# Low parts of whole weight rows by accumulating DMA, and products with the low part last, in a decoder layer on one core

## The chip, the core and the metric

The kernel runs on one core of a Trainium2 chip. The core has TensorE (matrix products into PSUM; PE in the rows), VectorE (DVE), ScalarE (ACT) and GpSimd (POOL), each with an instruction queue of its own, and SyncE (SP), which issues plain transfers. Transfers are carried by 16 DMA engines. The metric is the time of one execution on the device in microseconds (us).

## The reference

It is one step of one decoder layer, for 512 prompt tokens and 8 sample tokens that share their weights. Cut to its products:

```python
x = x + 0.5 * swiglu(rmsnorm(x, norm_ffn1), w_ffn1_gate, w_ffn1_up, w_ffn1_down)
z = rmsnorm(x, norm_mix) @ w_in
...  # RWKV-7 time mixing y_a, short convolution y_b, gates g_a and g_b, all from z
x = x + (g_a * y_a + g_b * y_b) @ w_out
x = x + 0.5 * swiglu(rmsnorm(x, norm_ffn2), w_ffn2_gate, w_ffn2_up, w_ffn2_down)
x = x + jax.nn.sigmoid(rmsnorm(x, norm_ple) @ w_ple_gate) * (p @ w_ple_proj)
```

Everything is float32; the model's width is 1024, that of the FFN 2816. A last norm follows.

## The kernel before

Tokens lie along the free dimension: 520 columns, handled as two halves of 260. The residual `X` is eight tiles of 128 x 520. A product's weights are blocks of 128 x 128; a whole row of 8 blocks is 128 x 1024 and takes in all of the model's width for 128 outputs.

**Three matmuls for one.** Float32 is worked out of two parts of TensorE's faster type fp32r: hi (rounded) and lo (what the rounding left). `mm3` (L171 to L173) does hi x h, hi x l and lo x h for one block, h and l being the parts of the activations (`xh`, `xl`; `xsh`, `xsl`; `th`, `tl`). A half of a product over a whole row is 8 blocks x 3 = 24 matmuls of 260 columns into one PSUM bank (`big`).

**How the parts are made.** `load` brings a row or block to `raw` through SP (L120). `make` (L122 to L132) then has two ways. With an engine in `eng`, ACT copies raw to hi (L130) and that engine subtracts: lo = raw - hi (L132). Without one, ACT writes -raw to lo (L128), a DMA that GpSimd issues adds the weights to it from HBM (L129), which leaves what the rounding of -raw lost, and ACT makes hi from raw.

**Whole rows.** `Row` is such a block of 128 x 1024; its raw, hi and lo tiles have two buffers each (tags raw8, hi8, lo8). `plain` (L212) builds a product from two units, one for each half of the columns; where the product is as deep as one row (`nk == NT`, 8 blocks) it uses one `Row`. These are wg1[1] and wu1[0 and 1] of FFN 1 (wg1[0] is prepared by hand in a tile of its own), w_out's rows 2 to 7, wg2[0 and 1] and wu2[0 and 1] of FFN 2, and the 8 rows of w_ple_gate (wpg): 21 in all. The other pairs of FFN rows go through `seven`, seven products of sums of blocks in place of eight; they take the sums `ts`, `th`, `tl` of the activations (`sums4`, L305 to L321), made by ACT and VectorE while the first products of an FFN run.

**What sets the order.** `run` (L184) walks through the units: it issues loads and `make` steps up to LEAD = 10 units ahead as the buffers allow, then a unit's matmuls, then what uses its result. Within this, a scheduler orders each engine's instructions by priorities and data. In FFN 1 and 2 the first result needs the norm's factors: `rstd` (L346) sums the squares on TensorE (`nsum`, L349), takes the root on ACT (`nR`, L350, behind a load of ACT's table) and the reciprocal on VectorE (L351).

Of the kernel before, what the change touches and what calls it, by code (L numbers as in the profile page):

```python
# [17 lines left out]
NT = 8  # L18
# [3 lines left out]
HN = N // 2  # L22
# [34 lines left out]
def hybrid_step(tc, I, O):  # L57
    nc = tc.nc
    from contextlib import ExitStack

    with ExitStack() as top:
# [34 lines left out]
        HALF = (slice(0, HN), slice(HN, N))  # L96
# [71 lines left out]
        def mm3(ps, b, i, x, first, last):  # L168

            hi, lo = b.hi[:, i, :], b.lo[:, i, :]  # L170
            nc.tensor.matmul(ps[:, :HN], lhsT=hi, rhs=x[0], start=first, stop=False, skip_group_check=True)  # L171
            nc.tensor.matmul(ps[:, :HN], lhsT=hi, rhs=x[1], start=False, stop=False, skip_group_check=True)  # L172
            nc.tensor.matmul(ps[:, :HN], lhsT=lo, rhs=x[0], start=False, stop=last, skip_group_check=True)  # L173
# [38 lines left out]
        def plain(pool, src, x, consume, mk=fps, lo_eng=None):  # L212

            nk = src.shape[1]
            if nk == NT:
                bs = [Row(src, nc.vector)]
            else:
                bs = [Blk(pool, src[:, k:min(k + KH, nk)], lo_eng) for k in range(0, nk, KH)]
            got = {}

            def half(j):
                def emit():
                    got[j] = mk("big")
                    k = 0
                    for b in bs:
                        for i in range(b.n):
                            a = x(k)
                            mm3(got[j], b, i, (a[0][:, HALF[j]], a[1][:, HALF[j]]), k == 0, k == nk - 1)
                            k += 1
                return emit  # L230
            n = len(bs)
            row = nk == NT
            if row:
                n = 0
            us = [Unit(half(0), lambda: consume(got[0][:, :HN], HALF[0]), bs, [b.make for b in bs], -n, n, 0, (row, row, row, 0)),
                  Unit(half(1), lambda: consume(got[1][:, :HN], HALF[1]), free=n, rows=(0, 0, 0, row))]
            for u in us:
                u.used = consume
            return us
# [146 lines left out]
        def ffn(fp, wg, wu, wd, XS, TS, R, htile, post):  # L386
# [79 lines left out]
            def down(m, k0, n, mk=mwps):  # L466
                last = k0 + n == NF

                def on_d(ps, cs):
                    nc.vector.scalar_tensor_tensor(X[m][:, cs], ps, 0.5, X[m][:, cs], ALU.mult, ALU.add)  # L470
                    if last and m == NT - 1:
                        post(m, cs)
                    elif last and cs.start:
                        post(m, ALL)
                return plain(fp, wd[m][:, k0:k0 + n], lambda k: hs[k0 + k], on_d, mk, nc.vector if k0 == 0 and m < KH else None)

            units, downs = [], []
            for q in range(NPAIR):
                f = 2 * q
                if q == 0:  # L480
                    parts = [plain(fp, w[f + i], lambda k: XS[k], on(q, i)) for w, on in ((wg, on_g1), (wu, on_u1)) for i in range(2)]
                else:
                    parts = [seven(fp, w[f], w[f + 1], XS, TS, on(q), nc.vector if q == 1 else None) for w, on in ((wg, on_g), (wu, on_u))]
                for x in parts:
                    units += x
                    if q:
                        for _ in range(2):
                            if downs:
                                units += downs.pop(0)
                if q % 2 and q < NPAIR - 3:  # L490
                    downs += [down(m, f - 2, 4) for m in range(NT)]
                elif q == NPAIR - 2:

                    downs += [down(m, f - 2, 4) for m in range(KH)]
# [151 lines left out]
        with tc.tile_pool(name="f2", bufs=1) as fp:  # L646
# [50 lines left out]
            def plains(w, x, on):  # L697
                us = [u for m in range(NT) if w[m] is not None
                      for u in plain(fp, w[m], x, lambda ps, cs, m=m: on(ps, cs, m))]
                us[-1].now = us[-2].now = True  # L700
                return us
# [779 lines left out]
```

## Time and profile before

| what | value |
|---|---|
| time, median of 3 runs | 1517.29 us (1516.64 to 1518.45) |
| the profiled execution | 1518.29 us, of which its span is 1516.5 |
| mean granted clock of TensorE | 0.977 of full speed |
| busy share of the span: TensorE, VectorE, ACT, GpSimd | 95%, 71%, 51%, 26% |
| FFN 1, the mix, w_out, FFN 2, wpg begin at about | 5, 350, 1044, 1090, 1453 us |

The span runs from the first to the last instruction; the 1.8 us beside it belong to the launch. The profiled execution is 1.0 us above the median of the runs.

### The profile page before, as it was taken

Reading aid. Unit: us, or ns where it says so; the run is one execution under the profiler, and the core shown is the slowest. Engines: PE = TensorE matmul, PEld = TensorE weight load, DVE = VectorE, ACT = ScalarE, POOL = GpSimd, SP = SyncE. Lnnn points to the kernel's source line nnn. Section 1 sums busy time; section 2 is a strip of 40 time slices with the busy share of each in tenths; the row PEclk is TensorE's granted clock in tenths of the full one; section 3 lists DMA queues with packets and bytes.
Section 4 is the critical chain, followed back from the end, with each engine's and each line's share of the span. In section 5 each row is a group of like instructions: output and inputs, shape, how many; then the busy total and the mean of one; then the engine's idle time right before and its main releaser. Section 6 shows DMA issues by size and latency. Waiting matters only on the chain.

```text
span 1516.5 us, 36191 instructions
## 1 busy us (share of the span) xinstructions
PE 1446.9 (95%) x14772; PEld 1390.4 (92%) x14772; DVE 1076.5 (71%) x2349; ACT 770.1 (51%) x1352; POOL 398.5 (26%) x447
## 2 busy tenths in 40 slices
PE   8799999999999999999899999998989999999996
PEld 7799999999988988989888897898979999999996
DVE  7976665665698877859887659855697665666566
ACT  7655555555633443634444352244475555555643
POOL 1324334334231211201320113311023334333401
PEclk9899999999998999999999999999999999999998
DMA  5678888888332322313222222325246887888823
GB/s 180 153 167 182 181 183 183 182 191 181 123 106 68 82 66 53 97 45 83 67 67 66 73 78 87 100 88 168 91 125 161 178 185 176 192 180 172 169 68 103
DMA packets 116709, 193.44 MB, mean 128 GB/s; under 512 B 41992, under 2 KB 51208, under 8 KB 116288
## 3 DMA queue, kind: packets, MB, share of 16 engines
q1 hardware_dynamic: 92928, 140.80, 30.4%
q0 software_dynamic: 23616, 50.34, 20.7%
q8 instruction: 116, 1.90, 0.5%
q14 instruction: 49, 0.40, 0.1%
HBM read 179.83 MB, written 11.01 MB: 126 GB/s over the span
## 4 chain that ended last, share of the span: by engine, by line
PE 75%; DVE 15%; ACT 3%; issue 3%; DMA 2%; POOL 1%; SPq 0%; DVEq 0%; ACTq 0%; POOLq 0%
PE big L171 16%; PE big L173 16%; PE big L172 16%; PE big L795 6%; PE big L796 6%; PE big L797 5%; DVE lo L132 2%; PE xy L1171 1%; PE ds L1186 1%; PE xy L1177 1%; ACT hi L130 1%; PE ft L1123 1%; PE xy L1154 1%; DVE F L1090 1%; ACT W L1127 1%
## 5 line engine op out<-in xcount | busy, mean ns | idle before, releaser
L130 ACT ACTIVATE hi<-raw 128x512 fp32r<-128x512 f32 (+2 forms) x427 | 318.5, 749 | 323.6 <-PE big L172 171.2
L795 PE MATMUL big<-xh,hi 128*128 128x260 f32 x1040 | 310.5, 299 | 1.7 <-ACT cc L847 1.0
L797 PE MATMUL big<-xh,lo 128*128 128x260 f32 x1040 | 299.6, 289 | 2.0 <-DVE lo L132 2.0
L796 PE MATMUL big<-xl,hi 128*128 128x260 f32 x1040 | 300.8, 289 | 0.0
L132 DVE TENSOR_TENSOR lo<-raw,hi 128x512 fp32r<-128x512 f32 (+2 forms) x263 | 239.2, 912 | 62.1 <-ACT hi L130 57.0
L795 PEld LDWEIGHTS big<-xh,hi 128*128 128x128 f32 x1040 | 199.8, 192 | 11.6 <-ACT cc L847 1.2
L171 PE MATMUL big<-hh,hi 128*128 128x260 f32 x704 | 203.6, 289 | 3.0 <-DVE x L470 3.0
L797 PEld LDWEIGHTS big<-xh,lo 128*128 128x128 f32 x1040 | 199.3, 192 | 4.2 <-DVE lo L132 2.3
L796 PEld LDWEIGHTS big<-xl,hi 128*128 128x128 f32 x1040 | 200.1, 192 | 2.8
L172 PE MATMUL big<-hl,hi 128*128 128x260 f32 x704 | 199.5, 283 | 0.0
L173 PE MATMUL big<-hh,lo 128*128 128x260 f32 x704 | 199.5, 283 | 0.0
L171 PE MATMUL big<-th,hi 128*128 128x260 f32 x640 | 183.1, 286 | 8.5 <-ACT th L319 5.2
L172 PE MATMUL big<-tl,hi 128*128 128x260 f32 x640 | 182.8, 286 | 3.6 <-DVE tl L320 3.4
L173 PE MATMUL big<-th,lo 128*128 128x260 f32 x640 | 181.8, 284 | 0.0
L470 DVE SCALAR_TENSOR_TENSOR x<-big,x 128x260 f32<-128x260 f32 x176 | 74.5, 426 | 94.9 <-PE big L173 94.9
L171 PEld LDWEIGHTS big<-hh,hi 128*128 128x128 f32 x704 | 133.3, 189 | 6.5 <-DVE x L470 3.5
L173 PEld LDWEIGHTS big<-hh,lo 128*128 128x128 f32 x704 | 133.3, 189 | 0.0
L172 PEld LDWEIGHTS big<-hl,hi 128*128 128x128 f32 x704 | 133.2, 189 | 0.0
L171 PEld LDWEIGHTS big<-th,hi 128*128 128x128 f32 x640 | 121.5, 190 | 10.1 <-ACT th L319 6.0
L172 PEld LDWEIGHTS big<-tl,hi 128*128 128x128 f32 x640 | 121.6, 190 | 4.8 <-DVE tl L320 4.8
L171 PE MATMUL big<-xh,hi 128*128 128x260 f32 x400 | 114.9, 291 | 8.4 <-ACT hi L130 5.5
L166 DVE TENSOR_TENSOR raw<-raw 128x512 f32<-128x512 f32 x160 | 113.9, 713 | 12.6 <-DMA raw<-in_wu 5.6
(306 smaller groups left out, 3439.4 us busy)
## 6 DMA issues: line engine op xcount, KB each, us to landing
raw<-in_win SPq DMA_DIRECT2D x66, 512.0 KB, 3.8
raw<-in_wd SPq DMA_DIRECT2D x80, 256.0 KB, 2.9
lo<-in_wd POOLq DMA_DIRECT2D x72, 256.0 KB, 4.6
raw<-in_wu SPq DMA_DIRECT2D x24, 512.0 KB, 3.7
raw<-in_wg SPq DMA_DIRECT2D x23, 512.0 KB, 3.8
raw<-in_wg SPq DMA_DIRECT2D x40, 256.0 KB, 3.5
raw<-in_wu SPq DMA_DIRECT2D x40, 256.0 KB, 3.0
lo<-in_wg POOLq DMA_DIRECT2D x18, 512.0 KB, 5.7
```

Of the source, the lines that this page charges most:

```text
L130: nc.scalar.activation(self.hi[:, ks], self.raw[:, ks], AF.Identity)
L132: self.eng.tensor_tensor(self.lo[:, ks], self.raw[:, ks], self.hi[:, ks].bitcast(F32), ALU.subtract)
L166: nc.vector.tensor_tensor(self.raw, a.raw, b.raw, ALU.add)
L171: nc.tensor.matmul(ps[:, :HN], lhsT=hi, rhs=x[0], start=first, stop=False, skip_group_check=True)
L172: nc.tensor.matmul(ps[:, :HN], lhsT=hi, rhs=x[1], start=False, stop=False, skip_group_check=True)
L173: nc.tensor.matmul(ps[:, :HN], lhsT=lo, rhs=x[0], start=False, stop=last, skip_group_check=True)
L470: nc.vector.scalar_tensor_tensor(X[m][:, cs], ps, 0.5, X[m][:, cs], ALU.mult, ALU.add)
L795: nc.tensor.matmul(ps[:, :HN], lhsT=hi[:, k, :], rhs=hh[k][:, cs], start=k == 0, stop=False)
L796: nc.tensor.matmul(ps[:, :HN], lhsT=hi[:, k, :], rhs=hl[k][:, cs], start=False, stop=False)
L797: nc.tensor.matmul(ps[:, :HN], lhsT=lo[:, k, :], rhs=hh[k][:, cs], start=False, stop=k == nk - 1)
L1090: v1.tensor_tensor(f, f, ft[:, :, q0:, :j], ALU.add)
L1123: nc.tensor.matmul(ps[qd, i * 128:i * 128 + 96], lhsT=GM[qd, i, 96:], rhs=GM[qd, i, 0:96], start=False, stop=True, skip_group_check=True)
```

## The change

Two edits in `plain`, for products over a whole row alone. The `Row` gets no engine, so that its low part comes from ACT's copy of -raw and the accumulating DMA. And a half's 24 matmuls are written as 16 with the hi part (hi x h and hi x l for each of 8 blocks) and then 8 with the low part, in place of hi, hi, lo for each block. The number of matmuls is the same.

```diff
--- before.py
+++ after.py
@@ -213,7 +213,7 @@
 
             nk = src.shape[1]
             if nk == NT:
-                bs = [Row(src, nc.vector)]
+                bs = [Row(src)]
             else:
                 bs = [Blk(pool, src[:, k:min(k + KH, nk)], lo_eng) for k in range(0, nk, KH)]
             got = {}
@@ -221,6 +221,15 @@
             def half(j):
                 def emit():
                     got[j] = mk("big")
+                    if row:
+
+                        for part in range(2):
+                            for k in range(NT):
+                                h, l = (y[:, HALF[j]] for y in x(k))
+                                for w, r in (((bs[0].hi, h), (bs[0].hi, l)), ((bs[0].lo, h),))[part]:
+                                    nc.tensor.matmul(got[j][:, :HN], lhsT=w[:, k, :], rhs=r, start=part == k == 0 and r is h,
+                                                     stop=part == 1 and k == NT - 1, skip_group_check=True)
+                        return
                     k = 0
                     for b in bs:
                         for i in range(b.n):
```

Line numbers behind the second edit are 9 higher in the changed kernel (L304 there is L295 here). Numbers behind an underscore count tiles, and those of the two kernels differ.

**ACT at the start of FFN 1.** hi_164 and lo_165 are the parts of wg1[1]; hi_220 and lo_221 (before), or 221 and 222 (changed), those of wu1[0]; `nsq` are squares for the norm. Before:

```order
L130 ACTIVATE hi_164<-raw_135 128x1024
L342 ACTIVATE nsq_151<-x5_71 128x520
L130 ACTIVATE hi_220<-raw_162 128x1024
L342 ACTIVATE nsq_154<-x6_72 128x520
L342 ACTIVATE nsq_157<-x7_73 128x520
L350 ACT_TABLE_LOAD
L350 ACTIVATE nR_96<-nsum_256,vec_74 128x260
L350 ACTIVATE nR_96<-nsum_260,vec_74 128x260
L130 ACTIVATE hi_318<-raw_168 128x1024
```

With the change:

```order
L128 ACTIVATE lo_165<-raw_135 128x1024
L130 ACTIVATE hi_164<-raw_135 128x1024
L351 ACTIVATE nsq_151<-x5_71 128x520
L128 ACTIVATE lo_222<-raw_162 128x1024
L351 ACTIVATE nsq_154<-x6_72 128x520
L130 ACTIVATE hi_221<-raw_162 128x1024
L351 ACTIVATE nsq_157<-x7_73 128x520
L359 ACT_TABLE_LOAD
L359 ACTIVATE nR_96<-nsum_258,vec_74 128x260
L359 ACTIVATE nR_96<-nsum_262,vec_74 128x260
L130 ACTIVATE hi_320<-raw_169 128x1024
L128 ACTIVATE lo_321<-raw_169 128x1024
```

A copy for the low part now stands ahead of the one for hi, in the place that hi had, and two more such copies stand ahead of the norm's table load and of te.

**TensorE at the start of FFN 1.** The first matmuls of the second product (wg1[1]), whose two halves are big_230 and big_280 before, big_232 and big_282 with the change. Before:

```order
L171 MATMUL big_230<-xh0_97,hi_164 128x260
L172 MATMUL big_230<-xl0_98,hi_164 128x260
L171 MATMUL big_280<-xh0_97,hi_164 128x260
L172 MATMUL big_280<-xl0_98,hi_164 128x260
L173 MATMUL big_230<-xh0_97,lo_165 128x260
L171 MATMUL big_230<-xh1_99,hi_164 128x260
L172 MATMUL big_230<-xl1_100,hi_164 128x260
L173 MATMUL big_230<-xh1_99,lo_165 128x260
```

With the change, the last 2 of big_232's 16 hi matmuls and what follows them:

```order
L230 MATMUL big_232<-xh7_111,hi_164 128x260
L230 MATMUL big_232<-xl7_112,hi_164 128x260
L230 MATMUL big_282<-xh0_97,hi_164 128x260
L230 MATMUL big_282<-xl0_98,hi_164 128x260
L230 MATMUL big_282<-xh1_99,hi_164 128x260
L230 MATMUL big_282<-xl1_100,hi_164 128x260
L230 MATMUL big_282<-xh2_101,hi_164 128x260
L230 MATMUL big_232<-xh0_97,lo_165 128x260
L230 MATMUL big_232<-xh1_99,lo_165 128x260
```

And further on in the changed kernel, up to the norm's sums:

```order
L230 MATMUL big_232<-xh6_109,lo_165 128x260
L230 MATMUL big_232<-xh7_111,lo_165 128x260
L230 MATMUL big_282<-xl2_102,hi_164 128x260
L230 MATMUL big_282<-xh3_103,hi_164 128x260
L230 MATMUL big_282<-xl3_104,hi_164 128x260
L230 MATMUL big_282<-xh4_105,hi_164 128x260
L230 MATMUL big_282<-xl4_106,hi_164 128x260
L230 MATMUL big_282<-xh5_107,hi_164 128x260
L358 MATMUL nsum_258<-nss_95,vec_74 128x260
L358 MATMUL nsum_262<-nss_95,vec_74 128x260
```

Low parts were read from the fifth matmul of the product on; now 21 hi matmuls of both halves stand ahead of the first. The norm's sums stand behind 37 matmuls of the product before, and behind 35 with the change, 8 of them with the low part.

**ACT at the start of w_out.** hi_14409 (before) or hi_14412 (changed) is the hi part of w_out's row 2, hi_14415 or hi_14419 that of row 3; xsh and nsq are parts and squares of the residual. Before:

```order
L130 ACTIVATE hi_14409<-raw_14405 128x1024
L295 ACTIVATE xsh_14377<-x0_14199,vec_74 128x260 x2
L342 ACTIVATE nss_14375<-x0_14199 128x520
L295 ACTIVATE xsh_14377<-x1_14223,vec_74 128x260 x2
L342 ACTIVATE nsq_14398<-x1_14223 128x520
L130 ACTIVATE hi_14415<-raw_14407 128x1024
L295 ACTIVATE xsh_14379<-x2_14243,vec_74 128x260
```

With the change:

```order
L130 ACTIVATE hi_14412<-raw_14408 128x1024
L304 ACTIVATE xsh_14380<-x0_14202,vec_74 128x260 x2
L351 ACTIVATE nss_14378<-x0_14202 128x520
L304 ACTIVATE xsh_14380<-x1_14226,vec_74 128x260 x2
L351 ACTIVATE nsq_14401<-x1_14226 128x520
L128 ACTIVATE lo_14413<-raw_14408 128x1024
L128 ACTIVATE lo_14420<-raw_14410 128x1024
L130 ACTIVATE hi_14419<-raw_14410 128x1024
L130 ACTIVATE hi_14479<-raw_14417 128x1024
L304 ACTIVATE xsh_14382<-x2_14246,vec_74 128x260
```

The low copies of rows 2 and 3 stand between the squares and the hi copy of row 3. In TensorE's order, row 2's 32 hi matmuls are followed by 14 with hi_14419 and then by row 2's 16 with lo_14413; before, the low parts of row 2 were read from its fifth matmul on.

**ACT at the start of FFN 2.** hi_14885 (before) or hi_14896 (changed) is the hi part of wg2[1], hi_14985 that of wu2[0]; te begins the sums of the activations. Before:

```order
L130 ACTIVATE hi_14885<-raw_14738 128x1024
L350 ACT_TABLE_LOAD
L350 ACTIVATE nR_14376<-nsum_14864,vec_74 128x260
L350 ACTIVATE nR_14376<-nsum_14868,vec_74 128x260
L312 ACTIVATE te_14876<-x0_14199,vec_74 128x520
L312 ACTIVATE te_14876<-x4_14283,vec_74 128x520
L408 ACT_TABLE_LOAD
L408 ACTIVATE t_14863<-t_14863 128x520
L319 ACTIVATE th_14873<-ts_14875 128x1040
```

With the change:

```order
L130 ACTIVATE hi_14896<-raw_14748 128x1024
L128 ACTIVATE lo_14897<-raw_14748 128x1024
L359 ACT_TABLE_LOAD
L359 ACTIVATE nR_14379<-nsum_14875,vec_74 128x260
L359 ACTIVATE nR_14379<-nsum_14879,vec_74 128x260
L130 ACTIVATE hi_14985<-raw_14822 128x1024
L321 ACTIVATE te_14887<-x0_14202,vec_74 128x520
L321 ACTIVATE te_14887<-x4_14286,vec_74 128x520
L417 ACT_TABLE_LOAD
L417 ACTIVATE t_14874<-t_14874 128x520
```

A low copy has come in ahead of the table load, and hi_14985, which waits for a buffer of hi, stands ahead of te; before, the hi copy of that row (hi_14973) came later than the rows shown. VectorE's subtractions for these rows are gone from its order, and the sums' tl stand behind fewer subtractions and sums of blocks than before.

## Rows read from the trace of the kernel before

**Rows 1.** The page's first part, TensorE's row: busy us (share of the span), instructions.

```profile
PE 1446.9 (95%) x14772; PEld 1390.4 (92%) x14772; DVE 1076.5 (71%) x2349; ACT 770.1 (51%) x1352; POOL 398.5 (26%) x447
```

**Rows 2.** Busy us by stretch (instructions in brackets), granted clock, DMA share, GB/s.

```profile
19.00:21.00 2.00, 2.00 (x19) 2.00 (x18) 1.90 (x4) 1.05 (x2) 0.00 (x0) 1.00 1.07 340
42.00:60.00 18.00, 13.81 (x76) 12.61 (x77) 16.45 (x30) 10.96 (x18) 5.50 (x5) 0.64 0.58 147
1040.00:1062.00 22.00, 18.54 (x141) 18.13 (x140) 11.34 (x21) 8.67 (x14) 0.00 (x0) 0.92 0.44 137
1470.00:1496.00 26.00, 26.00 (x219) 26.00 (x219) 19.06 (x31) 12.47 (x18) 0.00 (x0) 1.00 0.37 113
```

**Rows 3.** Groups by form: instruction, count | busy us, mean ns | idle before.

```profile
L132 DVE TENSOR_TENSOR lo<-raw,hi 128x1024 fp32r<-128x1024 f32 x93 | 116.5, 1253 | 37.7 <-ACT hi L130 36.3 <-PE ft L1123 0.7
L128 ACT ACTIVATE lo<-raw 128x1024 fp32r<-128x1024 f32 x36 | 37.6, 1044 | 0.6 <-PE big L173 0.6
```

**Rows 4.** Timeline, a low copy: start us, us, instruction [idle before <-releaser].

```profile
45.29 1.06 ACT L128 ACTIVATE lo<-raw 128x1024 fp32r<-128x1024 f32 x1 [0.56 <-PE big L173]
46.66 0.87 POOL L129 DMA_DIRECT2D lo<-in_wg  x1 [0.60 <-ACT lo L128]
```

**Rows 5.** The page's DMA queues and issues; accumulating landings, 0:60 and 1121:1123.

```profile
q1 hardware_dynamic: 92928, 140.80, 30.4%
q0 software_dynamic: 23616, 50.34, 20.7%
lo<-in_wg POOLq DMA_DIRECT2D x18, 512.0 KB, 5.7
...
DMA to landing us min/median/max: 4.0/4.2/6.0
...
DMA to landing us min/median/max: 7.3/7.3/7.3
```

**Rows 6.** Timeline of the start of FFN 1, same columns.

```profile
14.52 1.04 ACT L130 ACTIVATE hi<-raw 128x1024 fp32r<-128x1024 f32 x1
21.36 0.70 PE L349 MATMUL nsum<-nss,vec 128*128 128x260 f32 x2
22.61 3.41 DVE L351 RECIPROCAL nR<-nR 128x260 f32<-128x260 f32 x2 [1.31 <-ACT nR L350]
28.25 2.33 DVE L132 TENSOR_TENSOR lo<-raw,hi 128x1024 fp32r<-128x1024 f32 x1
49.33 1.24 DVE L320 TENSOR_TENSOR tl<-ts,th 128x1040 fp32r<-128x1040 f32 x1 [0.19 <-ACT th L319]
49.35 0.58 PE L171 MATMUL big<-th,hi 128*128 128x260 f32 x1 [3.17 <-ACT th L319]
```

**Rows 7.** Timeline of the start of w_out.

```profile
1048.25 1.04 ACT L130 ACTIVATE hi<-raw 128x1024 fp32r<-128x1024 f32 x1
1048.48 0.59 PE L173 MATMUL big<-xh,lo 128*128 128x260 f32 x1 [3.15 <-DVE lo L132]
1051.03 0.42 PE L172 MATMUL big<-xl,hi 128*128 128x260 f32 x1
1051.25 0.42 PE L173 MATMUL big<-xh,lo 128*128 128x260 f32 x1
1061.12 1.06 ACT L130 ACTIVATE hi<-raw 128x1024 fp32r<-128x1024 f32 x1 [1.55 <-PE big L172]
```

**Rows 8.** Timeline of the start of FFN 2.

```profile
1090.49 0.47 PE L171 MATMUL big<-xsh,hi 128*128 128x260 f32 x1
1092.77 3.41 DVE L351 RECIPROCAL nR<-nR 128x260 f32<-128x260 f32 x2 [0.57 <-ACT nR L350]
1105.26 1.21 DVE L132 TENSOR_TENSOR lo<-raw,hi 128x1024 fp32r<-128x1024 f32 x1
1122.51 0.39 PE L172 MATMUL big<-tl,hi 128*128 128x260 f32 x1 [0.89 <-DVE tl L320]
1140.81 0.39 PE L171 MATMUL big<-th,hi 128*128 128x260 f32 x1 [1.79 <-DVE u L441]
```


## The prediction

> **What bounds the kernel now.** The page's first part says it at once: TensorE's matmuls are busy 95% of the span [rows 1]. The table of busy time by stretch says where the rest is lost: in the middle of the row products nothing is (26.00 us busy of 26, 219 matmuls, so 0.119 us each), while at the starts of the stages TensorE stands still and the clock falls (a granted clock of 0.64 in 42 to 60, 0.92 in 1040 to 1062) [rows 2]. So work taken from VectorE is worth nothing in the middle of these products; it can be worth something only where TensorE waits: at the start of FFN 1, of w_out and of FFN 2. Since about 1,515 of the 1,517 us are untouched, the question is what happens at three starts, and whether the new transfers keep up in between.
>
> **The pieces and their prices.** Removed: 21 subtractions of 128x1024 on VectorE, 1253 ns each (26 us). Added: 21 ACT copies of 128x1024, 1044 ns each (22 us) [rows 3], and 21 accumulating transfers of 512 KB issued by GpSimd. Neither total is on the path by itself: VectorE is busy 71% of the span and ACT 51%. What counts is how long a low part takes from its raw row. Before, ACT copy and VectorE subtraction: 1.04 + 1.22 us. After: the ACT copy of -raw, a lag of 0.31 us to GpSimd's issue (46.66 against 45.29 + 1.06) [rows 4], and the landing. For 512 KB the page gives a median of 5.7 us from issue; singly I see 4.0 to 6.0 in the first 60 us and 7.3 in a busy stretch [rows 5]. I take 5.7, or 6.0 where other loads run beside it, and keep 4.0 and 7.3 as ends. Then a low part is there about 7.1 us after its ACT copy starts, 4.8 us later than before. The new order hides 16 of a half's 24 matmuls (1.9 us) of that; prefetching must hide the rest.
>
> A sentence from the Trainium skill bears on this price ("DMA: Bandwidth & Descriptors", section "Anatomy of one DMA — SWDGE (gpsimd) path"): it fits such a transfer as 2.0 us plus its bytes over 436 thousand per us, from which I work out an estimate of 3.2 us for 512 KB. The trace's 5.7 us does not agree; by the page, low parts would come some 2.5 us earlier and the sum below would be that of the second rival.
>
> **A, start of FFN 1.** Product 0 is untouched. Of product 1, 37 matmuls stand ahead of the norm's sum in the order of before, 35 in that of the change, but 14 of these come behind the first low part. Before: the sum ran at 21.36, and VectorE's reciprocal, from which a nearly gapless VectorE chain runs to the last tl at 49.33, began at 22.61; TensorE then still waited 3.17 us at 49.35 for that chain [rows 6]. After: ACT makes lo_165 at the place where it made hi (14.52), so it ends at 15.57 and the transfer is issued at 15.9; with 6.0 us it lands at 21.9 (the DMA engines are all taken from 19 to 21: share 1.07 [rows 2]). hi_164 comes at 16.6, just as product 0 ends. TensorE does 21 matmuls of it, to 16.6 + 21 x 0.12 = 19.1, and waits 2.8 us. After a wait of 3.15 us at w_out the next 13 matmuls came 0.216 us apart, the step of 1.2 GHz [rows 7]; I price the 14 matmuls here so: 3.0 us. The sum runs at 24.9, 3.5 us late, and so does the VectorE chain. That chain has lost one subtraction (28.25, 2.33 us, the usual price 1.22): 1.7 between. A = 3.5 - 1.7 = **+1.8 us**. Ends: a landing of 4.0 gives 19.9, a short wait, no fall of the clock, the sum 0.2 late, A = -1.5; 7.3 gives the sum 4.9 late and A = +3.7.
>
> **B, start of w_out.** Before, TensorE did 4 matmuls, waited 3.15 us for VectorE's subtraction (queued behind the residual adds) and ran 13 at half speed [rows 7]; the second product ended at about 1061.0 (the ACT copy that waits for it starts at 1061.12). After, it goes on where it stopped (1048.48 - 3.15 = 1045.3) with the 28 other hi matmuls of that product, to 1045.3 + 28 x 0.12 = 1048.7. Then it needs hi_14419, which now stands third in ACT's row, behind lo_14413 and lo_14420: 1048.25 + 3 x 1.05 = 1051.4, a wait of 2.7. The 14 matmuls that come ahead of the first low part, at 0.216, bring it to 1054.4. lo_14413 lands at 1049.3 + 0.3 + 5.7 = 1055.3: another 0.9. The 50 matmuls left take 6.0 at full clock: 1061.3, or 1062.3 if the clock stays down for some ten of them. B = **+0.8** (0.3 to 1.3); with 4.0 there is no second wait, -0.7; with 7.3 +2.5. So a stall of some 3 us is not removed: it changes its owner, from VectorE to ACT.
>
> **C, start of FFN 2.** The reciprocal starts as before (the ACT low copy stands where hi stood, and hi starts a little earlier). te, which followed the norm's scales at once, now stands behind hi_14985. This waits until the hi matmuls of the product of 1090.49 are through, 40 matmuls (4.8 us) later, and takes 1.05: te at about 1096.4. VectorE is in its reciprocals until 1096.2, so this costs it 0.4 to 0.9. It loses the subtraction of 1105.26 (1.21 us), and others move behind tl, so that the last tl, for which TensorE waited until 1122.51, comes up to 3.6 us earlier. But what was moved back must still be done: the next wait, 1.79 us at 1140.81 for VectorE's u, is gated by the whole backlog [rows 8]. I therefore count only what left the chain, and the wins at the waits: **-1.2**, between +0.5 (te's delay counts) and -2.8.
>
> **D, the rows in between.** The row tiles have two buffers. lo of product p+2 may begin when product p ends; the copy (1.05), the lag (0.3) and 0.1 of signalling leave, up to the 17th matmul of p+2 (5.76 + 1.92 = 7.7 us later), 6.2 us for the landing. 5.7 fits with half a us to spare. GpSimd does nothing else in w_out and wpg (1470 to 1496: 0.00 busy [rows 2]), so no issue is held up. DMA room: the accumulating queue took 20.7% of 16 engines for 50.34 MB, the plain one 30.4% for 140.80 MB [rows 5]; that is 6.2 us per MB against 3.3, so 3.3 us per row of 512 KB and, for a whole wpg product with its raw row (1.7) and pq (0.9), about 5.9 of 5.76 us if all ran at once; before, loads ran far ahead (share 0.37). That is tight: I add **+0.5** for a few late landings. If every one took 7.3, the cycle of a buffer (32 matmuls, 3.84, + 1.45 + 7.3 = 12.6 us for two products, not 11.52) costs 0.54 a product, over some 12 products +6.5.
>
> SP's queue hardly moves, TensorE's matmuls stay the same in number, and the end of the kernel (behind 1496) isn't touched.
>
> **Sum.** +1.8 + 0.8 - 1.2 + 0.5 = +1.9 us on the profiled execution, 1518.29 us, gives 1520.2; it ran 1.0 above the median 1517.29, so against the median I forecast **1519.2**.
>
> **The rivals.**
>
> *The transfers don't keep up* (slower): all landings like the 7.3 us: A +3.7, B +2.5, C +0.5, D +6.5, together +13, 1530; at 6.7 about half that. For it: the DMA arithmetic of D. Against: wpg moved little before, and quiet stretches gave 4.0. Beside it stands a warning of the Trainium skill ("SBUF — State Buffer", section "SBUF: two separate sides"): VectorE in its two-port modes keeps GpSimd from writing descriptors for transfers it issues; that would lengthen landings, and no row of before isolates it.
>
> *The transfers are early* (faster, the other side): decided at the start of FFN 1. If lo_165 lands within about 4.3 us of its issue, TensorE hardly waits, the clock holds, and the subtraction that left VectorE's chain is a gain: A -1.5, B -0.7, C -2.8, D 0, together -5, 1512.3. For it: two of the three landings in the first 60 us took 4.0 to 4.2. Against: those ran when the DMA engines had room, and 19 to 21 is full.
>
> *It cancels*: VectorE's spare time in 42 to 60 (1.55 us of 18) takes up most of A's delay, A about +0.3, and C gets -1.5: +0.1, 1517.4.
>
> **Chances.** A measurement of this kernel can tell about 0.2% (3 us) from no change. Forecast +1.9 (own range 1517.5 to 1522): 0.45. Late transfers: 0.17. Early ones: 0.18. Cancelling: 0.20. Of the forecast's cases a quarter pass +3 us; of the early ones some stay above -3 us, of the late ones a few below +3. So slower 0.28, same 0.55, faster 0.17. For 8 in 10 the range takes in the early case (1512.3) almost whole and the milder half of the late one: 1512.5 to 1525.
>
> **What would show it.** A: a wait of 2 to 3 us before the 22nd hi matmul, for a DMA, the clock below full from 21 to 25, the reciprocal near 26. B: a wait for ACT's hi at about 1048.4 to 1051.4, one of 1 us for a DMA behind it. C: last tl before 1121, the wait for u still there. D: TensorE full from 1450 to 1496. The forecast is wrong if accumulating landings sit away from 5 to 6 us, if the clock doesn't fall after A's wait, or if TensorE waits in wpg.

## The result and the profile after

The change made the kernel slower: 1543.65 us (median of 6 runs, 1535.16 to 1544.17) against 1517.17 us before on the same chip, a ratio of 1.0158 (95% interval 1.0139 to 1.0176; the two medians alone give 26 us, 1.0175). The forecast, 1519.2 us with a range up to 1525, missed. The profiled execution, 1535.16 us, is the quickest of the six; a second one (`after_again`, below) took 1542.95.

The page after, first the row of the engines and the two DMA queues (columns as in [rows 1] and [rows 5]), then the accumulating transfers of the two stages that had none before:

```profile
PE 1446.6 (94%) x14772; PEld 1389.9 (91%) x14772; DVE 1053.0 (69%) x2328; ACT 789.7 (51%) x1373; POOL 416.9 (27%) x468
...
q1 hardware_dynamic: 92928, 140.80, 29.8%
q0 software_dynamic: 26640, 61.35, 24.4%
...
lo<-in_wpg POOLq DMA_DIRECT2D x8, 512.0 KB, 6.7
lo<-in_wo POOLq DMA_DIRECT2D x6, 512.0 KB, 7.9
```

TensorE is busy for as long as before, and its mean granted clock is 0.977 in both profiles; VectorE lost 23.5 us, ACT gained 19.6. So, in sum, the time lost is waiting. The first rows of TensorE's waits by what ended them, over the whole span (us in total, times, longest):

```profile
PE big L230 <- DMA lo<-in_wo: 7.8, 3, 3.1
...
PE big L230 <- DMA lo<-in_wpg: 5.7, 2, 5.6
PE big L230 <- DMA lo<-in_wg: 5.7, 2, 4.5
PE big L230 <- DMA lo<-in_wu: 5.5, 3, 2.8
```

These are 24.7 us of waits for an accumulating DMA; before there was none. The loss is smaller than that because waits of before, the 3.15 us of [rows 7] above all, are gone or shorter. Where they stand, from the timeline of TensorE (FFN 1, w_out with its ACT wait, FFN 2, wpg):

```profile
23.08 0.59 PE L230 MATMUL big<-xh,lo 128*128 128x260 f32 x1 [4.49 <-DMA lo<-in_wg]
...
1051.35 0.39 PE L230 MATMUL big<-xh,hi 128*128 128x260 f32 x1 [1.96 <-ACT hi L130]
1056.36 3.47 PE L230 MATMUL big<-xh,lo 128*128 128x260 f32 x16 [3.08 <-DMA lo<-in_wo]
1069.22 1.23 PE L230 MATMUL big<-xh,lo 128*128 128x260 f32 x8 [2.98 <-DMA lo<-in_wo]
...
1122.55 3.84 PE L230 MATMUL big<-xsh,lo 128*128 128x260 f32 x16 [2.83 <-DMA lo<-in_wu]
...
1499.59 2.10 PE L230 MATMUL big<-xs,lo 128*128 128x260 f32 x8 [5.56 <-DMA lo<-in_wpg]
```

Behind the longer waits the clock falls to the lower of its two levels, 1.2 GHz: the 16 matmuls of 1056.36 took 3.47 us, 0.22 each, and the 8 of 1499.59 2.10, where the 8 of 1069.22 took 1.23. Behind the wait of 2.98 us the fall came 1.3 us later, and behind that of 1.96 there was none. The stretches behind 1056.36 and 1069.22 (columns as in [rows 2]; the granted clock is the third number from the end):

```profile
1056.30:1060.00 3.70, 3.64 (x18) 3.61 (x18) 0.55 (x2) 0.64 (x2) 0.00 (x0) 0.57 0.90 239
1071.00:1072.00 1.00, 1.00 (x6) 1.00 (x6) 0.49 (x1) 0.46 (x1) 0.00 (x0) 0.50 0.95 209
```

By stages, from the first start of each stage's marker on TensorE (the norms' sums, the first matmul of w_out's own products in the mix, wo), in us:

| run | to FFN 1's sum | to the mix's first group sum | to wo | wo to FFN 2's sum | to wpg's sum | to the end |
|---|---|---|---|---|---|---|
| before | 21.4 | 364.8 | 645.5 | 58.1 | 369.1 | 57.6 |
| after | 26.2 | 363.4 | 642.8 | 68.8 | 366.4 | 65.8 |
| `after_again` | 26.7 | 365.0 | 646.8 | 69.9 | 366.4 | 66.4 |
| `e1_order` | 21.4 | 366.6 | 646.3 | 54.7 | 367.9 | 57.7 |

The first profile's 16.9 us are +4.8, -1.4, -2.7, +10.7, -2.7 and +8.2. The mix, which the change leaves alone, takes 642.8 to 646.8 us from one profile to the next. Of the 7.8 us between the two profiles of the changed kernel 4.0 lie there, so differences of a few us between single profiles are not put down to an edit below unless its own stage shows them.

### The profile page after: what moved, and what is told of

It reads as the page before. It is cut to its first block, busy times and chain, and to the rows that moved or that the text cites. A ratio compares the mean times of both kernels' runs of the same rounds, so it can differ in the third digit from the quotient of the medians.

```text
span 1533.4 us, 36253 instructions
## 1 busy us (share of the span) xinstructions
PE 1446.6 (94%) x14772; PEld 1389.9 (91%) x14772; DVE 1053.0 (69%) x2328; ACT 789.7 (51%) x1373; POOL 416.9 (27%) x468
## 4 chain that ended last, share of the span: by engine, by line
PE 38%; DVE 6%; issue 6%; DMA 5%; ACT 2%; POOL 1%; DVEq 0%; POOLq 0%; ACTq 0%
PE big L171 7%; PE big L172 7%; PE big L173 7%; PE big L804 4%; PE big L805 4%; PE big L806 4%; DMA lo<-in_wo 1%; DMA lo<-in_wpg 1%; PE big L230 1%; PE xy L1180 1%; PE ds L1195 1%; DVE lo L132 1%; PE xy L1186 1%; PE xy L1163 1%; DMA lo<-in_wu 1%
## 5 line engine op out<-in xcount | busy, mean ns | idle before, releaser
L804 PE MATMUL big<-xh,hi 128*128 128x260 f32 x1040 | 309.9, 298 | 1.0 <-ACT cc L856 1.0
L132 DVE TENSOR_TENSOR lo<-raw,hi 128x512 fp32r<-128x512 f32 (+2 forms) x242 | 212.8, 882 | 46.1 <-ACT hi L130 40.9
L128 ACT ACTIVATE lo<-raw 128x512 fp32r<-128x512 f32 (+2 forms) x185 | 134.7, 730 | 1.0 <-PE big L230 0.8
```

The costliest lines, as they stand in the source:

```text
L128: nc.scalar.activation(self.lo[:, ks], self.raw[:, ks], AF.Identity, scale=-1.0)
L132: self.eng.tensor_tensor(self.lo[:, ks], self.raw[:, ks], self.hi[:, ks].bitcast(F32), ALU.subtract)
L804: nc.tensor.matmul(ps[:, :HN], lhsT=hi[:, k, :], rhs=hh[k][:, cs], start=k == 0, stop=False)
```

## The experiments

Times are ratios to the kernel before on the same chip. Landing means from GpSimd's issue to the end of the transfer.

### One half of the change alone, the load held back, the change again

Theory L: the same ACT copy that starts an accumulating transfer frees the raw tile, so that a plain load starts with it, and the landing is late. The rivals: the transfer is slow by itself; or the order of the matmuls costs.

```diff
# e1_order
-                bs = [Row(src)]
+                bs = [Row(src, nc.vector)]
# e2_dma_mixed
-                    if row:
+                    if False:
# e3_hold: the make step of a whole row
+            def make_hold():
+                b = bs[0]
+                b.make()
+                nc.gpsimd.tensor_copy(b.raw[:, 0, 0:1], b.lo[:, 0, 0:1].bitcast(F32))
```

> Only the new order of the matmuls; low parts of these rows by VectorE's subtraction as before. If the accumulating transfers are the whole cost, this is not slower than before: at w_out the low part comes at 1048.4 and 28 more hi matmuls stand ahead of it, so the wait of 3.15 us shrinks to the one for ACT's hi of row 3 (about 0.6), and the 13 matmuls at half speed go: about 1513 us (1511 to 1517). If the order itself costs (the norm's sums behind more matmuls, rows of hi read sooner), it is slower than before: 1519 or more.

> Only the accumulating DMA; matmuls in the old order hi, hi, lo. If late landings are the cost, the 1.7 us that the order had hidden are lost on top: a buffer of low parts then turns in 5.76 + 1.45 + 7.5 = 14.7 us for two products, where the change needs 12.8, so about 1 us more for each of 12 products and more at the starts: 1550 to 1565 us. If the order were the cost, this is between before and the change: 1520 to 1535.

> The change, but the next plain load of a whole row starts only when the accumulating transfer has landed (GpSimd copies one column of the low part into the raw tile, after its last reader). Theory: the ACT copy that starts an accumulating transfer also frees the raw tile, so a plain load of 512 KB starts with it and takes its share of the engines; then landings in w_out and wpg fall from 7 to 8 us to 4.0 to 5.5, the DMA waits there fall under 1 us each, and the time is about 1525 us (1520 to 1530). Rival, the accumulating transfer is slow by itself in these stretches: landings stay at 7 or more, and the time at 1535 to 1545.

> The changed kernel unaltered, for a second profile, since its runs lay between 1535 and 1544 us. If the difference comes from landings, the stretch that is longer shows longer waits for the accumulating DMA (wpg, where one wait of 5.6 us stood, above all); if it comes from the mix, which gave back 4 us of FFN 1's delay in the first profile, the shift at w_out's start is 4 to 5 us here instead of 0.7.

Measured: the order alone **0.9972** (0.9961 to 0.9984), faster than before; the DMA alone **1.0332** (1.0308 to 1.0357), a median of 1568.96 us where I had expected 1550 to 1565; the load held back 1.0175 (1.0160 to 1.0190); the change again 1.0134 (1.0108 to 1.0161). The order is not the cost; it gives 4 us back. The waits in w_out (1040 to 1092) of the order alone, against [rows 7]:

```profile
PE big L230 <- DVE lo L132: 0.5, 1, 0.5
PE big L230 <- ACT hi L130: 0.3, 1, 0.3
```

The 3.15 us stall is down to 0.5, as 28 more hi matmuls cover VectorE's subtraction. And the order hides a part of the DMA's lateness: without it the DMA costs twice as much (0.0332 over before, against 0.0162 over the order alone).

Holding the load back did half of what L says. In 1062 to 1078, landings of the change and, below, of `e3_hold`:

```profile
DMA to landing us min/median/max: 7.8/8.0/8.0
```

```profile
DMA to landing us min/median/max: 5.5/5.5/5.6
```

but no time was won in all. In `e3_hold` w_out's stretch took 65.9 us, some 3 less than with the change, but the two behind it took 373.6 and 70.0, 7 and 4 more. The held loads came late themselves and lay beside later transfers (landings of up to 8.8 in wpg), and GpSimd waits for each landing in its row; how much of FFN 2's 7 us that wait is was not traced. The time is the rival's, though the landings fell as L says. So the next runs take the load away instead of moving it.

### wpg: the plain load, the buffers, ACT's row

```diff
# e4_noload: wpg's rows 2 to 7 take the raw tiles of rows 0 and 1
+                if self.like is not None:
+                    self.raw = self.like.raw
# e6_three: hi and lo of wpg in three places each (the places are left out here)
-                    if nm > i and (nm > i + LEAD or prep + m.preps > PREP or raw + m.raws > RAW or rprep + m.rows[2] > 2):
+                    if nm > i and (nm > i + LEAD or prep + m.preps > PREP or raw + m.raws > RAW or rprep + m.rows[2] > (3 if m.own else 2)):
# e10_nosq: e4_noload, and
+                    if m in (0, NT - 1):
                         nrm3.add(m, c)
# e13_pq2: e4_noload, and
-                    keep["q"] = fp.tile([P, 2, N], F32, tag="u", name="pq", bufs=1)[:, 0]
+                    if m == 0:
+                        keep["u"] = fp.tile([P, 2, N], F32, tag="u", name="pq", bufs=1)
+                    keep["q"] = keep["u"][:, m % 2]
```

> The change, but wpg's rows 2 to 7 do not load their plain row (they take the raw tiles of rows 0 and 1 again, so six rows of w_ple_gate are not the right ones); the accumulating transfers stay. If the plain load that starts with it makes the landing late, the landings in wpg (5.1 to 8.3 us) fall to 4 to 5, no wait for them over 1 us stays, and the stretch from wpg's norm sum to the end takes 58 to 60 us in place of 66: the time is 6 to 8 us under the changed kernel's. If the accumulating transfer is slow by itself, landings of 6.5 to 8 and the 66 us stay.

> The change, but with three buffers for hi and low parts in wpg (in tiles that are idle by then), so that a row's ACT copy and transfer can start one product sooner. If the landing is only too late (two buffers leave it 6.2 us), the waits in wpg go although landings stay at 6 to 8 us, and the stretch from wpg's norm sum to the end takes 58 to 60 us in place of 66. If the DMA engines are full (2.9 us of all engines for a low row, 1.7 for the raw row, 0.9 for pq, of 5.76), the waits only move, and 63 to 66 us stay.

> As the run without plain loads in wpg, and the squares of rows 1 to 6 for the last norm are left out there (so the last norm's factors are wrong), with which ACT waited for VectorE's residual ahead of a low copy. One wait of 3.3 us was left in that run. If ACT's queue is its cause, the low copies start as soon as the buffer is free, no wait for a landing over 0.5 us is left in wpg, and the stretch from wpg's norm sum to the end takes 57 to 59 us in place of 62.8. If not, the 3.3 us wait stays.

> As the run without plain loads in wpg, with two places for pq in place of one, so that pq is loaded a product earlier. Theory: a low copy was late because it stands in ACT's row behind an operation (nsq, fo) that waits for VectorE's residual, and this waits for pq, whose load starts late and shares the engines with the low part; then VectorE does not wait over 1 us for pq here, no wait for a low part over 0.5 us is left in wpg, and the stretch from wpg's norm sum to the end takes 57 to 59 us (62.8 with one place). Rival: the low part's own landing of 5.5 us is too long; the wait of 3.3 us stays.

The stretch from wpg's sum to the end: the change 65.8 and 66.4, `e4_noload` 62.8, `e10_nosq` 64.2, `e13_pq2` **57.9**, `e6_three` **57.9** (57.6 before). The ratios: 1.0120, 1.0128 (two runs), 1.0095 (two runs) and 1.0103. In `e4_noload` the transfer's low part holds, beside the rounding, the difference between the two rows.

Landings issued in 1465 to 1510, the change first, `e4_noload` below:

```profile
DMA to landing us min/median/max: 5.1/5.9/8.3
```

```profile
DMA to landing us min/median/max: 5.3/5.5/5.7
```

Without the load every landing is one of 5.3 to 5.7 us, longer than the 4 to 5 I expected, and one wait of 3.27 us was left, so that 62.8 missed the 58 to 60 expected. ACT's row shows why, already in the change itself (timeline of ACT, then of VectorE and GpSimd):

```profile
1485.45 1.06 ACT L130 ACTIVATE hi<-raw 128x1024 fp32r<-128x1024 f32 x1
1489.38 0.64 ACT L351 ACTIVATE nsq<-x 128x520 f32<-128x520 f32 x1 [2.86 <-DVE x L700]
1489.92 1.05 ACT L128 ACTIVATE lo<-raw 128x1024 fp32r<-128x1024 f32 x1
...
1487.85 0.70 DVE L699 TENSOR_TENSOR ts<-ts,pq 128x520 f32<-128x520 f32 x1 [1.94 <-DMA pq<-ppd]
...
1491.26 0.86 POOL L129 DMA_DIRECT2D lo<-in_wpg  x1 [8.34 <-ACT lo L128]
```

The low copy could start at about 1486.5, behind hi. It stands behind nsq, which waits for VectorE's residual, which waits for pq, a load that shares the DMA engines. So it starts 3.4 us late, its landing takes 8.3 us, and TensorE waits 5.56. Leaving nsq out (`e10_nosq`) did not help: fo, the next operation that waits for the residual, took its place (a wait of 4.5 us). Loading pq a product earlier did: in 1470 to 1512 the waits of `e13_pq2` are

```profile
PE big L239 <- DMA lo<-in_wpg: 0.9, 2, 0.7
```

and `e6_three` has none at all in the same stretch, with landings of 5.5 to 7.2 there. So the DMA engines have room for wpg over a whole product; the transfers only come too late for two buffers. Of wpg's 8.2 us, the load makes up 3.0 (65.8 to 62.8) and pq's late start 4.9 more (to 57.9); pq earlier with the loads kept was not run.

### w_out: buffers, the start, and the plain load

```diff
# e11_three2: e6_three, and three places in w_out
-  own=(fp, m) if on is on_p else None
+  own=(fp, m - 2 * (on is on_o), on is on_o)
# e12_three_f1dve: and FFN 1 by VectorE
+                bs = [Row(src, None if own or stage[0] == "f2" else nc.vector)]
# e14_start_dve: and w_out's rows 2 and 3 by VectorE
+                None if own and not (own[2] and own[1] < 2) or stage[0] == "f2" else nc.vector
# e17_wo_four: the order everywhere, the DMA in w_out's rows 4 to 7 alone
+                bs = [Row(src, None if stage[0] == "wo" and wos.count("wo") > 2 else nc.vector)]
# e16_wo_noload: e17_wo_four, rows 4 to 7 with the raw tiles of rows 2 and 3
# (rows 2 and 3 get raw tiles of their own; that part is left out here)
+                    if len(wos) > 2:
+                        b.like = wos[-3]
```

> The change with three buffers for hi and low parts in wpg and also in w_out. If two buffers' 6.2 us for a landing are the cost there too, the stretch from w_out's own products to FFN 2's norm sum (58.1 us before, 68.8 and 69.9 with the change) takes 59 to 63, wpg 58, and the time is 1.002 to 1.007 of before. If w_out's cost is its start (ACT's two low copies ahead of hi, the first landing), at least 66 us stay there, and the time is 1.008 or more.

> The same with three buffers, and FFN 1's three rows by VectorE: no late first landing. If late landings were all that the accumulating DMA cost, 0.995 to 1.000 of before, and what VectorE no longer does in w_out and wpg brings nothing over the order alone (0.9972) or the order with FFN 2's rows by DMA (0.9962), since TensorE did not wait for VectorE there. If the transfers cost more than their landings (w_out's start, the engines' time), 1.002 or more.

> As the run with three buffers and FFN 1 by VectorE (1.0064 of before), and w_out's rows 2 and 3, the first two, by VectorE as well. If that kernel's remaining 14 us over the order alone stand at the start of w_out (ACT's low copies ahead of hi, the first landing of 8 us, the half clock behind it), the stretch from w_out's own products to FFN 2's norm sum falls from 64.9 to 55 to 58 us and the time to 0.996 to 0.999 of before. If the transfers cost time elsewhere, it stays above 1.002.

> The new order everywhere; the accumulating DMA for w_out's rows 4 to 7 alone, its first two rows and all others by VectorE. This leaves out the start of w_out and all other stages. By the changed kernel's trace the waits of 2.98 and 1.73 us behind landings of 7.3 to 8 us remain, with the half clock behind them: 5 to 7 us over the order alone, the stretch from w_out's own products to FFN 2's norm sum 59 to 62 us (54.7 with the order alone), the time 1.000 to 1.003 of before. If these waits came from the start, 55 to 57 us and 0.996 to 0.998.

> The same, but rows 4 to 7 of w_out load no plain row (they take the raw tiles of rows 2 and 3 again; the low part that the transfer makes then holds the difference to the right row too, more coarsely rounded). If the plain load beside it is what makes a landing late, landings are 5 to 6 us, no wait of over 0.5 us for them is left in w_out, and the stretch takes 55 to 57 us: 0.996 to 0.999 of before. If not, it is as long as with the loads.

| run | ratio (95% interval) | wo to FFN 2's sum | landings in w_out |
|---|---|---|---|
| `e11_three2` | 1.0095 (1.0072 to 1.0117) | 65.3 | 7.1 to 11.2 |
| `e12_three_f1dve` | 1.0064 (1.0046 to 1.0082) | 64.9 | 7.2 to 11.0 |
| `e14_start_dve` | 1.0052 (1.0032 to 1.0073) | 62.3 | 7.2 to 10.8 |
| `e17_wo_four` | 1.0021 (1.0007 to 1.0035) | 59.2 | 7.3 to 8.3 |
| `e16_wo_noload` | 0.9973 (0.9960 to 0.9987) | 54.9 | 5.4 to 6.3 |
| `e1_order`, no DMA | 0.9972 (0.9961 to 0.9984) | 54.7 | none |

Three buffers cured wpg but not w_out, a miss of mine: in w_out they let accumulating transfers run two at a time beside the raw loads, landings of up to 11 us, and the waits moved (one of 4.44 us in `e14_start_dve`). VectorE at the start took away only 2.6 us where I had expected 7 or more. The last pair settles it for w_out. Landings issued in 1050 to 1078, `e17_wo_four`, then `e16_wo_noload`:

```profile
DMA to landing us min/median/max: 7.3/7.8/8.3
```

```profile
DMA to landing us min/median/max: 5.4/5.6/6.3
```

With the loads TensorE waits four times (1.19, 0.67, 0.79 and 0.33 us), without them never for a low part, and the stretch is as long as with no DMA at all. In `e16_wo_noload` no plain row is issued from 1046 to 1079: as rows 2 and 3 have raw tiles of their own, FFN 2's first rows are loaded ahead of it. TensorE's waits in 1040 to 1098, and the engines in 1056 to 1084 (columns as in [rows 2]), again with the loads first:

```profile
PE big L233 <- DMA lo<-in_wo: 3.0, 4, 1.2
...
1056.00:1084.00 28.00, 25.02 (x202) 24.16 (x201) 11.90 (x23) 15.11 (x23) 3.47 (x4) 1.00 0.75 164
```

```profile
PE big L249 <- ACT hi L130: 1.5, 1, 1.5
...
1056.00:1084.00 28.00, 27.92 (x232) 27.70 (x231) 13.55 (x27) 15.66 (x24) 3.47 (x4) 1.00 0.53 95
```

The DMA engines are not full on average even with the loads (0.75), but while TensorE waits they are: 1.01 in 1053 to 1056.3 of the change. The other cause that the late rival named, VectorE holding up GpSimd's descriptors, is not what differs in this pair: VectorE is busier where the landings are shorter (13.55 us against 11.90), and GpSimd's four issues take 3.47 us in both.

That the load is released with the transfer is seen in the change (ACT, SP and GpSimd, at two products):

```profile
1074.88 1.06 ACT L128 ACTIVATE lo<-raw 128x1024 fp32r<-128x1024 f32 x1
...
1075.97 0.33 SPq L120 DMA_DIRECT2D raw<-in_wg  x1
...
1076.23 0.86 POOL L129 DMA_DIRECT2D lo<-in_wo  x1 [9.64 <-ACT lo L128]
...
1089.46 0.33 SPq L120 DMA_DIRECT2D raw<-in_wu  x1
...
1089.72 0.86 POOL L129 DMA_DIRECT2D lo<-in_wg  x1 [6.90 <-ACT lo L128]
```

The low copy ends at 1075.94. It was the raw tile's last reader: 0.03 us later SP issues the next load into it, and 0.26 us after that GpSimd issues the accumulating transfer. A plain load stands so, 0.26 to 0.28 us ahead, at nine of the ten transfers of w_out and FFN 2.

### The FFNs alone

```diff
# e5_f2, e8_f1, e15_best: the order everywhere, the DMA where stage[0] is in DMA
+                bs = [Row(src, None if stage[0] in DMA else nc.vector)]
```

> The new order everywhere, the accumulating DMA in FFN 2's four rows alone. In the changed kernel FFN 2, from its norm sum to wpg's, was 2.7 us shorter than before; the order alone made it 1.2 shorter. If VectorE's relief is the gain, this is 1 to 2 us faster than the order alone: 0.995 to 0.997 of before. If the four landings of 7.4 to 8.6 us cost more than that (the first of them lies in w_out), it is 2 us or more slower than the order alone, 0.999 or more.

> The new order everywhere, the accumulating DMA in FFN 1's three rows alone. If the late first landing is carried to the end (the norm's sum 4.8 to 5.3 us late in both profiles of the change), this is about 5 us slower than the order alone: 1.000 to 1.002 of before. If VectorE's lost subtraction and its spare time take it up, as the prediction had it, at most 2 us: 0.998 or less.

> The new order everywhere, and the accumulating DMA for FFN 1's two wu1 rows and FFN 2's four rows. wg1[1], whose late landing held the first norm, goes by VectorE. If VectorE's relief helps where its chain to tl is what TensorE waits for, 1 to 3 us faster than with FFN 2 alone: 0.994 to 0.996 of before. If the landings of 7.5 to 9 us in FFN 1 cost as much, 0.996 to 0.998.

FFN 2 alone: **0.9962** (0.9950 to 0.9975), the fastest kernel of the study, though its interval overlaps that of the order alone. FFN 1 alone: 0.9988 (0.9978 to 0.9998), between the two answers: FFN 1's sum is 5.2 us late there (26.6), but by the ratios the end is some 2.4 us over the order alone (0.0016 of 1517; the two intervals overlap). `e15_best` missed: 1.0000 (0.9983 to 1.0017); its first wu1 row is waited for (1.79 us at 26.37).

## Why the prediction was wrong, point by point

**The step that failed** is the landing: "I take 5.7, or 6.0 where other loads run beside it", and with it D's "5.7 fits with half a us to spare". The landings were 7.9 and 9.0 us in FFN 1's first two, 6.6 to 9.5 in w_out, 7.4 to 8.6 in FFN 2's four and 5.1 to 8.3 in wpg. The median came from `seven`'s rows, whose raw row the sums of blocks still read when the low copy is made. In `plain` nothing reads the raw row any more, so in w_out and FFN 2 a plain load of 512 KB starts with the transfer, and `e16_wo_noload` shows what that costs. In FFN 1 the low copy stands ahead of hi, and plain loads start 0.7 and 1.1 us behind the first transfer; no run took them away, so what made those two landings late is not shown. I had added up the engines' time for both (D) but not asked when each starts. The estimate of 3.2 us for 512 KB, worked out from the fit of the Trainium skill ("DMA: Bandwidth & Descriptors", section "Anatomy of one DMA — SWDGE (gpsimd) path"), was further off: 5.3 to 5.7 with no such load, so that its rival, early transfers, is out. The accumulating queue's packets took 60 us more than before for 21 rows, 2.9 us of all engines each, against 1.7 for a plain row by [rows 5].

**A, +1.8.** The late sum was right in kind and at my upper end: TensorE waited 4.49 us at 23.08, and the reciprocal came at 27.31, 4.7 late; I had 3.5 for 6.0 us and 4.9 for 7.3. The landing was 7.9, beyond my end, but its transfer went out at 15.1, 0.8 us earlier than I had it, so the two errors partly cancel. Of the 1.7 us given back 0.7 came by the wait for th (49.35 before, now 53.36), and they were gone again at the wait for u, which ended at 68.97 before and now at 73.73. `e8_f1` puts the net at some 2.4 us by its ratio; what gives the rest back further on was not traced.

**B, +0.8.** The ACT wait at 1051.35 (1.96 us, 2.7 foretold) and the second wait behind it were right, but not their sizes: the 14 matmuls between them ran at full clock (1051.35 to 1053.28, the second wait's start), and lo_14413 landed 6.6 us after its issue, so that the second wait was 3.08 us in place of 0.9. The half clock came behind that one.

**C, -1.2.** Right in sign and within its bounds: -2.7 in both profiles. But the order alone gives 1.2 of that (367.9 in `e1_order`), which C did not have; the other 1.5 came with the DMA (366.4 in `e5_f2` too). The last tl starts 29.1 us behind the norm's sum, 31.4 before.

**D, +0.5** was the large miss: with the first waits of w_out, its later ones and wpg +18.9 us where B and D together had 1.3. Its rule, 6.2 us of room, held: a landing of 6.3 made no wait in `e16_wo_noload`, while in `e17_wo_four` the first, of 7.3, made one of 1.19 us. Those behind it, of 7.7 to 8.3, made only 0.33 to 0.79 us of wait, since each wait also moves the next row's use back. The rival "the transfers don't keep up" was the case that came, with a chance of 0.17 and 1530; it was right that landings of 7.3 us and more keep TensorE waiting, but its price was 13 us where it was 17 and 25 in the two profiles and 26 by the medians. Two things were missing from it: in wpg the low copy starts 3.4 us late behind nsq, which no step looked at (I followed the buffer, not what stands ahead in ACT's row), and the longer waits cost the half clock on top (16 matmuls in 3.47 us at 1056.36). And "the DMA engines are full" over a whole product was not the reason: three buffers hid it all in wpg. In w_out, overlapping transfers made the landings longer with three buffers; what would hide them there was not found.

**The order of the matmuls** I had priced only with the DMA. Alone it is worth 4 us, as `e1_order` shows, at the very stall of [rows 7] that I said would only change its owner.

## What to carry to other kernels

When a step goes from an engine to a DMA, ask what the operation that starts it also releases: here it freed the buffer that the next load waited for, and both shared the engines, so that 5.5 us became 8. Take a landing time only from transfers started in the same way, and count the room for it from when the starting operation really runs, with all that stands ahead of it on its engine. A new order that puts the late operand last is worth trying by itself, without the slower way of making that operand.

## What the runs showed of the hardware

- An accumulating transfer of 512 KB landed 5.3 to 5.7 us after its issue with pq beside it (`e4_noload`), and 5.4 to 6.3 with no plain row issued beside it (`e16_wo_noload`). With a plain load of 512 KB issued 0.26 to 0.28 us ahead of it, it took 7.7 to 8.3 in `e17_wo_four` and 6.2 to 8.6 in the change.
- On average over the 21 rows its packets take 2.9 us of all 16 engines for 512 KB, 1.7 times a plain load's time. The Trainium skill ("DMA: Bandwidth & Descriptors", section "Rules for kernel authors") says that an accumulate reads its destination and writes it later; the longer time agrees with that, though no row shows the read by itself.
- The mix, unchanged, took 642.6 to 646.9 us between the same two marks in the eighteen profiles.
